# Where a feed-forward pass adds its residual: sixteen half tiles moved from the end of the fourth block to the up projections of the second

## The chip, the cores and the metric

The kernel runs on one core of a Trainium2 chip. The metric is device time in microseconds of one execution; the time before is the median of three runs, 2182.12 us (2181.38 to 2185.97). Five engines work side by side, each through a queue of its own and in that queue's order: TensorE (PE; its weight loads are listed as PEld), VectorE (DVE), ScalarE (ACT), GpSimd (POOL) and SyncE (SP), which here only issues DMA transfers. ACT and POOL can issue transfers too.

## The reference

One layer of an encoder trunk on a sequence of 2048 tokens with 1024 features, float32:

```python
mix, qx = spatial_gating_mixer(x, a_w_in[j], a_v_ln_g[j], a_v_ln_b[j], a_w_s[j], a_b_s[j])
branch = jnp.concatenate([mix, memory_cross_attention(qx, mem, w_mem_kv[i])], axis=-1)
x = layer_norm(DEEPNORM_ALPHA * x + branch @ w_o[i], ln1_g[i], ln1_b[i])
x = layer_norm(DEEPNORM_ALPHA * x + swiglu_ffn(x, ffn_w_in[i], ffn_w_down[i]), ln2_g[i], ln2_b[i])

def swiglu_ffn(x, w_in, w_down):
    h = x @ w_in
    return (jax.nn.silu(h[..., :D_FF]) * h[..., D_FF:]) @ w_down
```

D_FF is 2816, DEEPNORM_ALPHA is 2 to the power 1/4. The change concerns the term `DEEPNORM_ALPHA * x` of the last line, the residual of the feed-forward part (FFN).

## The kernel before, in words

Features lie on the 128 partitions and tokens along the free axis. The first part (mixer, attention, first norm) runs over four chunks of 512 tokens and leaves its result in a DRAM tile `x1d`. Each float32 operand is split into a high part (an ACT cast, L73) and a low part (a DVE subtraction, L74), and each product is three matmuls: high by high, high by low, low by high.

The FFN runs in three passes over 688, 680 and 680 tokens. The 22 tiles of 128 hidden features are taken in five blocks, in passes 1 and 2 of 4, 4, 4, 4 and 6. A block has two stages:

- The up projections (`Pass.up`, matmuls with output h), one for each hidden tile. Each is a seven-product scheme for two by two blocks: products in the order 1, 6, 2, 5, 7, 3, 4, each of 12 matmuls of 340 tokens, each with its own weight w. Four of the seven weights were kept split in DRAM in pass 0 and are loaded (`k_u`, from SP's queue); the other three are loaded as r_u and split anew. After each product comes a "stage" that reads the PSUM bank: L400 after products 1 (ACT) and 6 (DVE), L401 after 2 (ACT) and 5 (DVE), L402 after 7, L392 and others after 3 and 4. Products 3 and 4 go on accumulating in the banks that L401 and L402 have to read first. After a stage, `then` takes steps of generators handed in as `work`: the norm of the pass before (`norm_work`), and `pair`, which splits the results of two finished hidden tiles (gp).
- The down projection. In passes 1 and 2 the first four blocks go through `down7`, again in seven products, on pairs of hidden tiles (matmuls with output e, six to a product): for each of four pairs j of output tiles, products 6, 1, 5, 7 and then, one pair behind, `second` with products 2, 3, 4. DVE adds each product to the pass's accumulators `fa` or to a common term `fu` (L524); in the first block ACT writes some of them instead (L522). In the fourth block (`last`), `second` also adds `fu` to three quarters of the pair (L531, L532) and then the residual: for each of the two output tiles and each half of its tokens, a tile r of 128x340 is loaded from x1d on SP's queue (L539) into the pool `tmp` (nine buffers, which the up projections use as well), and DVE adds ALPHA times r (L541). The fifth block goes through `down` on split results g; then follow the norm and the store.

One up projection of the next block is made before a block's down stage (`ahead`), so four of them stand between the down stages of two blocks.

The order in each engine's queue is planned by the framework when the program is built: it goes by the order in which the program is written and by when it expects operands and buffers to be ready. An instruction can therefore stand in its queue far ahead of others that are written before it. The order of TensorE alone is fixed by hand.

The pool `ln` has one buffer each under the tags s1 and s2. The norm of the second half of a pass's tokens uses them for its sums: from the last down stage of its pass to the up projections of the next pass's first block. GpSimd makes those sums, and in pass 0 it also issues loads of r_es tiles (L481) and stores of weight sums for `left_sums`, a generator whose DVE operations (L493) run between the up projections of pass 0.

Of the kernel before, what the change touches and what calls it, by code (L numbers as in the profile page):

```python
# [11 lines left out]
F32 = mybir.dt.float32  # L12
F32R = mybir.dt.float32r
AF = mybir.ActivationFunctionType
ALU = mybir.AluOpType
AX = mybir.AxisListType

P = 128
# [8 lines left out]
KD = D // P  # L27
# [7 lines left out]
ALPHA = 2.0 ** 0.25  # L35
# [4 lines left out]
def trunk_kernel(ctx, tc, xT, memT, wv, wuq, ws, bs, vg, vb, wmk, wmv, wo,  # L40
                 ln1g, ln1b, w1, w2, ln2g, ln2b, outT):
    nc = tc.nc
# [16 lines left out]
    def matmul(*args, **kw):  # L59
        in_order(nc.tensor.matmul(*args, **kw))  # L60
# [4 lines left out]
    def bank(name):  # L65
        return psum.tile([P, 512], F32, tag="bank", name=name)
# [117 lines left out]
    x1d = dram.tile([D, SEQ], F32, tag="x1d", name="x1d")  # L184
# [108 lines left out]
    def norm_steps(norms, stores, wait, pad):  # L293

        for _ in range(wait):
            yield

        def pairs(call):
            for m in range(0, KD, 2):
                call(m, m + 2)  # L300
                yield

        for x in norms:
            yield from pairs(x.centre)
        for _ in range(pad):
            yield
        for x in norms:
            x.var()
            for _ in range(4):
                yield  # L310
        for _ in range(4):
            yield
        for x, store in zip(norms, stores):
            yield from pairs(lambda a, b: x.finish(store, a, b))
# [12 lines left out]
    open_pools = {}  # L327
# [17 lines left out]
    class Pass:  # L345
# [156 lines left out]
        def down7(self, blk, q, f0, last, w):  # L502

            h, n, gp = self.h, self.n, self.gp
            if blk == 0:
                self.u = [open_pools["sums"].tile([P, 4, P], F32, tag="sums", name=f"fu{self.no}_{m}")
                          .rearrange("p a b -> p (a b)")[:, 0:h] for m in range(0, KD, 2)]
            banks = []

            def product(j, p):  # L510
                y, u = self.out[j], self.u[j]
                c11, c12, c21, c22 = (y[:, a, b * h:(b + 1) * h] for a in range(2) for b in range(2))
                n, start, stop = {1: (0, True, False), 6: (1, True, True), 2: (0, False, True), 5: (2, True, False),
                                  7: (3, True, False), 3: (2, False, True), 4: (3, False, True)}[p]
                bk = banks[j][n]
                for i in range(q):
                    for x, (a, b) in enumerate(PASSES):
                        matmul(bk, w[j][p][:, a, i, :], gp[p][:, i, b], start=start and i == 0 and x == 0,
                               stop=stop and i == q - 1 and x == 2, skip_group_check=True)
                to = {1: u, 6: u, 2: c11, 5: c22, 7: c22, 3: c12, 4: c21}[p]  # L520
                if blk == 0 and p not in (1, 7):
                    nc.scalar.copy(to, bk)  # L522
                else:
                    nc.vector.tensor_add(to, to, bk)  # L524

            def second(j):
                for p in (2, 3, 4):
                    product(j, p)
                if last:
                    y, u = self.out[j], self.u[j]  # L530
                    nc.vector.tensor_add(y[:, 0, h:n], y[:, 0, h:n], u)  # L531
                    nc.vector.tensor_tensor(out=y[:, 1].rearrange("p (b t) -> p b t", b=2),  # L532
                                            in0=y[:, 1].rearrange("p (b t) -> p b t", b=2),
                                            in1=u.unsqueeze(1).broadcast_to([P, 2, h]), op=ALU.add)
                    for m in range(2):
                        m0 = (2 * j + m) * P
                        for x in range(2):
                            r, t0 = self.tmp(f"r{m}{x}_{j}"), self.t0 + x * h
                            nc.sync.dma_start(out=r, in_=x1d[m0:m0 + P, t0:t0 + h])  # L539
                            to = y[:, m, x * h:(x + 1) * h]  # L540
                            nc.vector.scalar_tensor_tensor(out=to, in0=r, scalar=ALPHA, in1=to,  # L541
                                                           op0=ALU.mult, op1=ALU.add)

            for j in range(KD // 2):
                if j < KD // 2 - 1:
                    w.append(self.left(blk, 2 * j + 2, f0, q))
                banks.append([bank(f"e{i}_{self.no}_{blk}_{j}")[:, 0:h] for i in range(4)])
                for p in (6, 1, 5, 7):
                    product(j, p)
                if j:  # L550
                    second(j - 1)
            second(KD // 2 - 1)

        def sums(self):

# [413 lines left out]
    late = chunks[-1]  # L969
# [8 lines left out]
    late.norm.squares = open_pools["sq"]  # L978
    ffn.rest()
    norm_work = norm_steps([late.norm], [late.store], 5, 5)  # L980
    sums_to_make = [(blk, m) for blk in range(4) for m in range(0, KD, 2)]
    for no in range(len(FPASSES)):
        pa, h, n = ffn, FPASSES[no] // 2, FPASSES[no]
        whole = (((h, n), (0, h)),)
        f0 = 0
        blocks = FBLOCKS[no]
        ahead = []

        side = []

        def up(f):
            work = [(norm_work, 1), *side]
            if no == 0 and f > 4 and sums_to_make:
                blk, m = sums_to_make.pop(0)
                work.append((pa.left_sums(blk, m, 4 * blk, 2), 1))
            ys = f, pa.up(f, work)
            for gen, _ in work[1:]:
                for _ in gen:
                    pass
            side.clear()  # L1000
            return ys

        for blk, nb in enumerate(blocks):
            end = blk == len(blocks) - 1
            fs = range(f0 + len(ahead), f0 + nb)
            if no and not end:
                ys = list(ahead)
                for f in fs:
                    ys.append(up(f))
                    if len(ys) % 2 == 0:  # L1010
                        side.append((pa.pair(len(ys) // 2 - 1, blk, ys[-2][1], ys[-1][1]), 2))
                ahead = [up(f0 + nb)]
            else:
                gs = [pa.whole(*y) for y in ahead] + [pa.whole(*up(f)) for f in fs]
                ahead = []
            seven = no and not end
            if seven:
                first = [pa.left(blk, 0, f0, nb // 2)]
            if blk == 0:
                for _ in norm_work:  # L1020
                    pass
                pa.sums()
            if seven:
                pa.down7(blk, nb // 2, f0, blk == len(blocks) - 2, first)
            elif not end:
                pa.down(blk, gs, f0, whole, lambda ci, m: None)
            elif no < len(FPASSES) - 1:
                ffn = Pass(no + 1)
                norms = [pa.norm(0, h), pa.norm(h, n)]

                def done(ci, m):
                    for i in range(2):
                        norms[i].add(pa.ya[m][:, i * h:(i + 1) * h])
                    if m % 2:
                        ffn.load(m // 2)

                pa.down(blk, gs, f0, whole, done)
                norm_work = norm_steps(norms, [pa.store(0, h), pa.store(h, n)], 6, 0)
            else:
                last = (((0, n - 256),), ((n - 256, n),))  # L1040
                norms = [pa.norm(0, n - 256), None]

                def done(ci, m):
                    if ci == 0:
                        norms[0].add(pa.ya[m][:, 0:n - 256])
                    elif m == 0:
                        norms[1] = pa.norm(n - 256, n, True)
                        norms[0].centre(0, 4)
                    else:
                        norms[1].add(pa.ya[m - 1][:, n - 256:n])  # L1050
                        if m == 1:
                            norms[0].centre(4, 8)
                        if m == 5:
                            norms[0].var()
                        if m == 7:
                            norms[0].spread()

                pa.down(blk, gs, f0, last, done)
                norms[1].add(pa.ya[KD - 1][:, n - 256:n])
                norms[1].centre_pairs()  # L1060
                norms[1].var()
                norms[1].spread()
                norms[0].finish(pa.store(0, n - 256))
                norms[1].finish(pa.store(n - 256, n))
            f0 += nb
# [54 lines left out]
```

## Time and profile before

| what | value |
|---|---|
| median of three runs | 2182.12 us |
| lowest and highest | 2181.38, 2185.97 us |
| profiled execution, its own time | 2188.79 us |
| its span | 2186.7 us |
| mean granted TensorE clock | 0.988 |
| busy share of PE, DVE, ACT, POOL | 96%, 73%, 42%, 17% |
| pass 1, first down stage to last up projection | 1320.9 to 1656.4 us |
| pass 2, the same | 1777.9 to 2113.2 us |

Times inside the profile count from the start of the span. A row of the timeline is start, length, engine, line, operation, output and inputs; in brackets stands how long the engine was idle before it, and what ended that. A row of a tile or line gives the number of instructions and their shortest, median and longest duration in ns. "To landing" is the time from the issue of a transfer until its data is there. The granted clock is TensorE's, as a share of full speed.

### The profile page before, as it was taken

How to read it: one execution, taken by the hardware profiler on the slowest of the kernel's cores; microseconds unless marked ns; L12 is line 12 of the kernel's file. 1: busy time of each engine (PE TensorE's matmuls, PEld its weight loads, DVE VectorE, ACT ScalarE, POOL GpSimd, SP SyncE). 2: the span in 40 equal slices, each digit the busy share in tenths (PEclk: the TensorE clock that was granted, in tenths of full speed). 3: DMA queues.
4: the chain of work that ended last, by engine and by line, in shares of the span. 5: the costliest groups of instructions: out<-in, count | busy, mean ns of one | idle time of the engine just before them, and what ended most of it. 6: DMA issues, size and time to landing. Idle time of an engine off the chain costs nothing.

```text
span 2186.7 us, 35143 instructions
## 1 busy us (share of the span) xinstructions
PE 2094.2 (96%) x12938; PEld 1982.2 (91%) x12938; DVE 1606.3 (73%) x3030; ACT 920.8 (42%) x1846; POOL 365.2 (17%) x318
## 2 busy tenths in 40 slices
PE   9899999999999989999999999999999999999896
PEld 7888798788888789999999999999999999999896
DVE  7986796797789796878778885656747755666656
ACT  5553653564474453434434354232224353223234
POOL 0412321331322450001000320000002300000002
PEclk9999999999999999999999999999999999999998
DMA  6233314234333556767668467666754576666652
GB/s 212 78 109 124 115 64 158 97 107 141 129 97 108 171 193 236 251 225 279 231 240 290 163 214 256 218 235 226 269 204 140 200 257 237 232 226 233 241 167 92
DMA packets 158604, 408.13 MB, mean 187 GB/s; under 512 B 15584, under 2 KB 46304, under 8 KB 158432
## 3 DMA queue, kind: packets, MB, share of 16 engines
q1 hardware_dynamic: 138112, 333.50, 45.4%
q10 hardware_dynamic: 12672, 46.14, 5.6%
q0 software_dynamic: 7648, 26.24, 3.4%
q8 instruction: 102, 1.67, 0.3%
q14 instruction: 70, 0.57, 0.1%
HBM read 326.13 MB, written 79.69 MB: 186 GB/s over the span
## 4 chain that ended last, share of the span: by engine, by line
PE 58%; DVE 19%; DMA 10%; ACT 5%; issue 5%; POOL 2%; SPq 0%; ACTq 0%; DVEq 0%; POOLq 0%
PE h L60 31%; PE e L60 9%; PE d L60 8%; PE v L60 5%; PE u L60 3%; DMA r_x<-in_xT 3%; DMA r_f<-x1d 2%; DMA r_es<-in_w 2%; DVE w L74 2%; DVE w_o L74 2%; DVE x L74 1%; DVE w_u L74 1%; POOL s_a L233 1%; ACT p L745 1%; DVE z L702 1%
## 5 line engine op out<-in xcount | busy, mean ns | idle before, releaser
L60 PE MATMUL h<-x,w 128*128 128x340 f32 (+1 forms) x5544 | 888.2, 321 | 37.3 <-DVE w L74 13.9
L60 PEld LDWEIGHTS h<-x,w 128*128 128x128 f32 x5544 | 874.6, 189 | 46.5 <-DVE w L74 15.8
L60 PE MATMUL d<-g,w_d 128*128 128x344 f32 (+3 forms) x1632 | 263.7, 322 | 6.0 <-DVE w_d L74 2.8
L60 PEld LDWEIGHTS d<-g,w_d 128*128 128x128 f32 x1632 | 257.8, 189 | 10.0 <-DVE w_d L74 3.7
L60 PE MATMUL y<-br,w_o 128*128 128x512 f32 x960 | 224.4, 395 | 0.0
L60 PEld LDWEIGHTS y<-br,w_o 128*128 128x128 f32 x960 | 180.4, 188 | 42.1
L60 PE MATMUL e<-gp,w_e 128*128 128x340 f32 x1344 | 211.4, 318 | 0.4 <-DMA w_e<-k_e 0.4
L60 PEld LDWEIGHTS e<-gp,w_e 128*128 128x128 f32 x1344 | 209.9, 188 | 0.8 <-DMA w_e<-k_e 0.7
L60 PE MATMUL v<-w_v,x 128*128 128x512 f32 x768 | 188.2, 401 | 6.6 <-ACT w_v L73 4.8
L73 ACT CAST w<-r_u 128x512 fp32r<-128x512 f32 x198 | 121.8, 618 | 168.2 <-PE h L60 125.0
L74 DVE TENSOR_TENSOR w<-r_u,w 128x512 fp32r<-128x512 f32 x198 | 143.4, 726 | 53.9 <-ACT w L73 46.7
L60 PEld LDWEIGHTS v<-w_v,x 128*128 128x128 f32 x768 | 143.8, 190 | 42.3 <-ACT w_v L73 4.8
L60 PE MATMUL u<-xt,w_u 128*128 128x256 f32 x768 | 97.1, 282 | 0.0
L60 PEld LDWEIGHTS u<-xt,w_u 128*128 128x128 f32 x768 | 94.3, 191 | 0.0
L60 PE MATMUL u<-x,w_u 128*128 128x256 f32 x576 | 79.4, 290 | 12.1 <-DVE u L711 6.2
L369 POOL TENSOR_TENSOR t<-r_f,r_f 128x340 f32<-128x340 f32 (+1 forms) x12 | 14.7, 1227 | 436.7 <-DMA r_f<-x1d 419.9
L60 PEld LDWEIGHTS u<-x,w_u 128*128 128x128 f32 x576 | 72.9, 193 | 14.7 <-issue 6.0
L400 DVE TENSOR_TENSOR u<-h,m 128x340 f32<-128x340 f32 (+1 forms) x66 | 33.7, 511 | 70.7 <-PE h L60 70.3
L73 ACT CAST gp<-c 128x340 fp32r<-128x340 f32 x112 | 51.7, 476 | 74.4 <-DVE c L398 42.0
L74 DVE TENSOR_TENSOR w_o<-r_o,w_o 128x512 fp32r<-128x512 f32 (+1 forms) x96 | 67.3, 712 | 21.0 <-ACT w_o L73 21.0
L73 ACT CAST w_d<-r_d 128x384 fp32r<-128x384 f32 (+2 forms) x104 | 53.2, 519 | 68.9 <-PE d L60 43.7
L74 DVE TENSOR_TENSOR w_d<-r_d,w_d 128x384 fp32r<-128x384 f32 (+2 forms) x104 | 61.9, 599 | 24.5 <-ACT w_d L73 24.3
(212 smaller groups left out, 2873.9 us busy)
## 6 DMA issues: line engine op xcount, KB each, us to landing
w<-k_u SPq DMA_DIRECT2D x176, 512.0 KB, 4.3
r_u<-in_w SPq DMA_DIRECT2D x88, 512.0 KB, 3.5
k_u<-w ACTq DMA_DIRECT2D x88, 512.0 KB, 3.9
r_u<-in_wuq SPq DMA_DIRECT2D x32, 512.0 KB, 3.3
r_o<-in_wo SPq DMA_DIRECT2D x32, 512.0 KB, 3.5
r_e<-in_w SPq DMA_DIRECT2D x64, 256.0 KB, 3.0
w_e<-k_e SPq DMA_DIRECT2D x64, 256.0 KB, 3.7
w_e<-k_e SPq DMA_DIRECT2D x32, 512.0 KB, 4.5
```

What stands on the lines that cost most here:

```text
L60: in_order(nc.tensor.matmul(*args, **kw))
L73: nc.scalar.copy(hi, src)
L74: engine.tensor_sub(lo, src, hi.bitcast(F32))
L233: nc.gpsimd.tensor_add(self.s2, self.s2, sq)
L369: nc.gpsimd.tensor_sub(t3, b22, b12)
L400: stages = {1: lambda: nc.scalar.copy(m1, q0), 6: lambda: nc.vector.tensor_add(u2, q1, m1), 2: lambda: nc.scalar.activation(m1, q0, AF.Sil ...
L702: nc.vector.tensor_scalar(z[h][:, b], z[h][:, b], mv[:, b, 0:1], rs[:, b:b + 1], ALU.subtract, ALU.mult)
L745: nc.scalar.activation(pr[:, h, :], svs[h // 2][:, h % 2, :], AF.Exp, scale=HD ** -0.5, bias=mxv[:, h:h + 1], accum_out=sm[:, h:h + 1])
```

## The change

The residual leaves `second` of the fourth block. A new generator `residual` loads each half tile from x1d on GpSimd's queue into the buffers s1 and s2 of the pool `ln` in turn, and adds ALPHA times it to the accumulator two loads later. It is created after the down stage of the first block, and one step of it is taken after each stage of the up projections that follow, behind the step of `norm_work`. Sixteen loads and two closing steps fit into the 28 stages of four up projections; what is left would be done ahead of the down stage of the third block. It holds for passes 1 and 2; pass 0 adds its residual with the first down products, as before.

```diff
@@ down7, second @@
-                    for m in range(2):
-                        m0 = (2 * j + m) * P
-                        for x in range(2):
-                            r, t0 = self.tmp(f"r{m}{x}_{j}"), self.t0 + x * h
-                            nc.sync.dma_start(out=r, in_=x1d[m0:m0 + P, t0:t0 + h])
-                            to = y[:, m, x * h:(x + 1) * h]
-                            nc.vector.scalar_tensor_tensor(out=to, in0=r, scalar=ALPHA, in1=to,
-                                                           op0=ALU.mult, op1=ALU.add)
@@ Pass @@
+        def residual(self):
+            h, late = self.h, []
+
+            def add():
+                to, r = late.pop(0)
+                nc.vector.scalar_tensor_tensor(out=to, in0=r, scalar=ALPHA, in1=to, op0=ALU.mult, op1=ALU.add)
+
+            for m in range(KD):
+                for x in range(2):
+                    if len(late) == 2:
+                        add()
+                    r = open_pools["ln"].tile([P, 432], F32, tag=f"s{1 + x}", name=f"res{self.no}_{m}_{x}")[:, 0:h]
+                    t0 = self.t0 + x * h
+                    nc.gpsimd.dma_start(out=r, in_=x1d[m * P:(m + 1) * P, t0:t0 + h])
+                    late.append((self.ya[m][:, x * h:(x + 1) * h], r))
+                    yield
+            while late:
+                add()
+                yield
@@ the loop over passes and blocks @@
+    residual = iter(())
...
-            work = [(norm_work, 1), *side]
+            work = [(norm_work, 1), (residual, 1), *side]
...
-            for gen, _ in work[1:]:
+            for gen, _ in work[2:]:
...
+            if blk == 2:
+                for _ in residual:
+                    pass
...
                 pa.down7(blk, nb // 2, f0, blk == len(blocks) - 2, first)
+                if blk == 0:
+                    residual = pa.residual()
```

## The prediction

> **What bounds the kernel now.** I read the page first, for the engine that sets the time.
>
> ```profile
> span 2186.7 us, 35143 instructions
> PE 2094.2 (96%) x12938; PEld 1982.2 (91%) x12938; DVE 1606.3 (73%) x3030; ACT 920.8 (42%) x1846; POOL 365.2 (17%) x318
> ```
>
> TensorE (PE) is busy 96% of the span, so a change pays only where PE stands still or runs slowly. The moved work sits in passes 1 and 2, at the end of their fourth block. There I read the chain of waits in order of time (start, length, what), from block 2 on.
>
> ```profile
> 1478.12 26.19 PE e L60 x168
> 1504.31 52.39 PE h L60 x336
> ...
> 1586.13 1.77 DVE fa L541 x4
> 1587.90 0.85 DVE g L74 x2
> 1588.75 0.61 DVE w L74
> 1589.41 61.62 PE h L60 x382
> ```
>
> Block 2 runs without a gap: 168 down products (e) in 26.19, then four up projections (h, 336 matmuls) in 52.39, so 0.1559 us a matmul. Block 3 does not: between e and h stand four residual adds (L541), two splits of g, and the split of the next weight w, which PE needs. The timeline of PE gives the sizes, pass 1 first, then pass 2 (start, length, what, and in brackets the idle time before it).
>
> ```profile
> 1556.54 10.46 PE L60 MATMUL e<-gp,w_e 128*128 128x340 f32 x66
> 1567.38 16.18 PE L60 MATMUL e<-gp,w_e 128*128 128x340 f32 x102 [0.38 <-DMA w_e<-k_e]
> 1583.39 0.47 PE L60 MATMUL h<-x,w 128*128 128x340 f32 x2
> 1589.41 67.21 PE L60 MATMUL h<-x,w 128*128 128x340 f32 x418 [5.55 <-DVE w L74]
> ...
> 2013.59 26.38 PE L60 MATMUL e<-gp,w_e 128*128 128x340 f32 x168
> 2039.81 0.47 PE L60 MATMUL h<-x,w 128*128 128x340 f32 x2
> 2045.82 67.57 PE L60 MATMUL h<-x,w 128*128 128x340 f32 x418 [5.54 <-DVE w L74]
> ```
>
> Each pass idles 5.5 us for that split. The stretches in time show a second loss (columns: length, then busy time of PE, PEld, DVE, ACT and POOL, granted clock, DMA share, GB/s).
>
> ```profile
> 1320.92:1347.14 26.22, 26.22 (x170) 26.22 (x170) 10.40 (x23) 13.09 (x31) 0.00 (x0) 1.00 0.70 235
> 1347.14:1399.52 52.38, 52.38 (x338) 52.38 (x338) 30.07 (x59) 18.28 (x39) 0.00 (x0) 1.00 0.67 232
> 1478.12:1504.31 26.19, 26.19 (x171) 26.19 (x170) 19.42 (x42) 5.08 (x12) 0.00 (x0) 1.00 0.66 219
> 1556.70:1583.60 26.90, 26.52 (x170) 26.22 (x169) 24.17 (x54) 5.37 (x13) 0.00 (x0) 1.00 0.92 297
> 1583.60:1589.40 5.80, 0.26 (x2) 0.00 (x0) 5.80 (x14) 0.00 (x0) 0.00 (x0) 0.75 0.65 254
> 1589.40:1593.40 4.00, 3.99 (x14) 3.99 (x15) 0.56 (x1) 0.44 (x1) 0.00 (x0) 0.51 0.36 131
> 2045.82:2049.82 4.00, 4.00 (x14) 4.00 (x15) 0.54 (x1) 0.44 (x1) 0.00 (x0) 0.50 0.36 131
> ```
>
> VectorE (DVE) is busy 24.17 of 26.90 in block 3's down stage and all of the 5.80 behind it: a backlog. For 4 us after the idle time the granted clock is half. DMA share is 0.92 there against 0.66 in block 2.
>
> **The cost of the stall as it stands.** Pass 1: idle 5.55; the 418 matmuls should take 418 x 0.1559 = 65.2 and took 67.2, so 2.0; the e stage from 1556.54 to 1583.39 is 26.85 against 26.19, so 0.7. Pass 2: 5.54, and 67.57 - 65.2 = 2.4; its e stage lost nothing. Together 8.2 + 7.9 = 16.1 us. This is the most that this part can return, 0.74%.
>
> [...]
>
> **Removed from block 3.** These rows are the residual tiles' own (durations in ns: least, median, most).
>
> ```profile
> L539 SPq DMA_DIRECT2D r<-x1d x32: 319/402/1167, 1557.3 to 2037.2; - x32
> L541 DVE SCALAR_TENSOR_TENSOR fa<-r,fa x32: 502/504/511, 1565.9 to 2043.8; 128x340 f32<-128x340 f32 x32
> DMA to landing us min/median/max: 3.1/4.8/6.1
> ```
>
> L539 is the load, L541 the add. Per pass, 16 loads leave SP's queue (16 x 0.40 = 6.4 us of issuing), 2.8 MB leave a stretch whose DMA share was 0.92, and 16 adds leave DVE. Overlapped, four adds take 1.77 us, so 0.44 each and 7.1 us in all. DVE's work from 1556.70 to the last split was 24.17 + 5.80 = 30.0 us; without the adds 22.9, against 26.2 us of PE. The backlog of 5.5 us is smaller than the 7.1 taken out. The 0.38 us wait for w_e, behind the r loads on SP's queue, goes too.
>
> What is late next: after the last product an add, the two u sums (L531 and L532), g and w still follow in before's order. The first row is L532's group within the backlog (count, busy time, mean ns); the second is a w split of block 2 on DVE's timeline.
>
> ```profile
> L532 DVE TENSOR_TENSOR fa<-fa,fu 128x680 f32<-128x680 f32 x1 | 0.9, 859 | 0.0
> ```
>
> ```profile
> 1497.70 0.69 DVE L74 TENSOR_TENSOR w<-r_u,w 128x512 fp32r<-128x512 f32 x1
> ```
>
> If w stays last, PE waits for 0.50 + 0.43 + 0.78 + 0.85 + 0.61 = 3.2 us less the 0.3 us of its two free matmuls, 2.9. If w is queued as in block 2, where it ran at 1497.70, 6.6 us ahead of the stage's end, PE waits for nothing. The queues aren't in program order (w is written after those products), and w goes into a gap of DVE. With 22.9 of 26.2 us used, block 3 has gaps as block 2 has (19.42). I take 0.9 a pass, one L532 ahead of w; bounds 0 and 2.9.
>
> **Added to the up projections of block 1.** POOL issues 16 loads a pass, where it has nothing else to do (0.00 busy in the stretch 1347.14:1399.52). At 546 ns, by the r_es row below, that is 8.7 us, and nothing is queued behind them: after the norm's last sums in block 0, POOL's next work is at the end of the pass.
>
> ```profile
> 1655.51 1.15 POOL L369 TENSOR_TENSOR t<-r_f,r_f 128x340 f32<-128x340 f32 x1 [376.61 <-DMA r_f<-x1d]
> ```
>
>  The buffers s1 and s2 are free by then: the norm that uses them ends in block 0. DVE gets 7.1 us, 30.1 + 7.1 = 37 of 52.4. DMA gets 2.8 MB on 12.2 MB (52.4 us at 232 GB/s), so the share goes from 0.67 to about 0.82; PE's weight loads bore 0.92 in block 3 with 0.38 us lost, so I take zero, bounds 0 and 0.4 a pass.
>
> The price is a wait on DVE. Two buffers serve 16 loads, so each buffer makes 8 rounds: add, load, landing, add. In program order an add stands two steps of 12 matmuls after its load, 2 x 1.87 = 3.74 us. If the load comes later, DVE, which runs in order, stands still, and PE's stages behind it too. Before has one like case: in pass 0, r_es tiles are loaded from GpSimd's queue and used by DVE between up projections.
>
> ```profile
> L481 POOL DMA_DIRECT2D r_es<-in_w x32: 543/546/576, 823.4 to 1176.5; - x32
>   DVE s_es L493: 9.0, 5
> DMA to landing us min/median/max: 3.8/6.7/8.9
> ```
>
> ```profile
> PE h L60 <- DVE c L401: 4.5, 4, 1.8
> ```
>
> There DVE waited 5 times in 16, 9.0 us in all, and PE lost 4.5 us, behind L401; 0.28 us a round. What DVE can wait without harm is seen in block 1's rows.
>
> ```profile
> 1354.65 0.51 DVE L401 TENSOR_TENSOR c<-h,u 128x340 f32<-128x340 f32 x1 [0.18 <-PE h L60]
> 1356.52 0.51 DVE L402 TENSOR_TENSOR c<-h,c 128x340 f32<-128x340 f32 x1 [1.35 <-PE h L60]
> ```
>
> Each must end before the product after next, 1.87 us after its start is possible: 1.87 - 0.51, less 0.2 for handing over (an estimate, from the 0.18 in the row), leaves 1.1 us. With landing at 4.8 (the r row) a round is 4.8 + 0.5 for the add + 0.1 = 5.4, 1.7 over the two steps and 0.6 over the slack. With 6.7 (the r_es row) it is 7.3, 2.4 over. With 3.1 nothing is lost. 8 rounds a pass lie between 0 and 8 x 2.4 = 19 us. I take r_es's 0.28 a round, since there DVE and PE stand in the same pattern and the queue is the same: 16 x 0.28 = 4.5 for two passes. Half of that falls away, as the first two loads have their buffers long before and the adds of early tiles can go into block 0's down stage, where DVE idles 26.22 - 10.40 = 15.8 us: 2.3.
>
> [...]
>
> **Sum.** 16.1 returned, less 2 x 0.9 at the tail, less 2.3 in the up projections: 12.0 us. The profiled execution took 2188.8 (2186.7 span), 0.3% above the median 2182.1 of the three runs; the difference carries over. 2182.1 - 12.0 = 2170.
>
> **The rivals.** (a) All of it comes back: w is early, and the loads are hidden in block 0 and the norm's free buffers. 2182.1 - 16.1 = 2166. For it: DVE's free 15.8 us; against: adds cannot precede their tiles, which end through the whole of block 0's down stage.
>
> (b) The change moves the backlog but w stays last in its queue. Then PE still waits 2.9 us a pass; 5.8 lost of 16.1, and 2.3 in the ups; if the clock also drops, 2.0 more a pass. 2174 to 2178. For it: the planned order of before put w behind all of DVE's late work. Against: three blocks of before put w ahead.
>
> (c) Slower: GpSimd's loads land late in every round, with all 16 in the up projections. One mechanism, DVE standing at the add with L401 or L402 behind it. At 7.3 us a round it costs 38 us and the kernel takes 2182.1 - 16.1 + 1.8 + 38 = 2206; if half the rounds go into block 0's stage, 2187. It decides at (16.1 - 1.8)/16 = 0.9 us lost a round, a landing of 0.9 + 1.1 + 3.74 - 0.6 = 5.1 us. For it: the r_es median lies above, and its rounds here come back to back. Against: r_es loads were queued behind 512 KB stores and each other, these are one at a time.
>
> (d) No change: the same mechanism with landings near 5.1 in all rounds, or near 6.0 in half of them: 2178 to 2186.
>
> **How the numbers follow.** Forecast 0.50; (a) 0.15; (b) 0.12; (d) 0.11; (c) 0.12. 0.2% of this kernel, 4.4 us, is about what a measurement can tell from no change. Forecast, (a) and (b) are faster, 0.77, of which I give 0.02 to the same: 0.75, 0.13, 0.12. The range goes from the full return, 2165, to 2183, leaving out (c) and the upper half of (d). The forecast's own range is 2167 to 2175.
>
> **What would show it.** Right: no gap over 1 us on PE between the fourth block's e stage and the next h in passes 1 and 2, the granted clock at 1.00 there, DVE's w split ahead of the last adds, and the up projections of block 1 at 52 to 55 us. Wrong: DVE idle with the residual load as its releaser before the new add, over 1 us each and many of them, with PE waiting on L401, L402 or w within 1347 to 1399 of pass 1 and the like stretch of pass 2; or the 5.5 us gap still there.

## The result: slower by 1%, and the profile after

The changed kernel takes 2203.45 us (median of four runs, 2202.19 to 2206.85) against 2183.97 us before; the ratio is 1.0097, 95% interval 1.0083 to 1.0111. In a later comparison it was 1.0085 (1.0070 to 1.0100). The forecast was 2170.

The profiled execution took 2202.19 us, its span is 2200.4. Work per engine is what it was: the page has PE at 2097.0 us busy (2094.2 before), DVE at 1607.9 (1606.3). What changed is where PE stands still. First the place that the residual left: the timeline of PE around the fourth block of pass 1 (start, length, what; idle time before it in brackets).

```profile
1569.23 26.38 PE L60 MATMUL e<-gp,w_e 128*128 128x340 f32 x168
1595.45 65.65 PE L60 MATMUL h<-x,w 128*128 128x340 f32 x420
1660.94 2.67 PE L60 MATMUL d<-g,w_d 128*128 128x340 f32 x16
```

No gap is left: 26.2 and 65.5 us where before had 26.9 and 73.1, and 26.2 and 65.4 in pass 2 (26.2 and 73.4 before). The two passes together got 16.3 us back. DVE's timeline shows why PE did not wait.

```profile
1589.93 0.69 DVE L74 TENSOR_TENSOR w<-r_u,w 128x512 fp32r<-128x512 f32 x1
...
1595.51 0.52 DVE L531 TENSOR_TENSOR fa<-fa,fu 128x340 f32<-128x340 f32 x1
1595.94 0.50 DVE L524 TENSOR_TENSOR fa<-fa,e 128x340 f32<-128x340 f32 x1
1596.47 0.87 DVE L532 TENSOR_TENSOR fa<-fa,fu 128x680 f32<-128x680 f32 x1
```

The split of w stands 5.5 us ahead of the stage's end, with the last adds and sums behind it. Now the place that the residual came to: the timeline of PE in block 1 of pass 1, then in pass 2.

```profile
1318.98 17.01 PE L60 MATMUL e<-gp,w_e 128*128 128x340 f32 x108
1336.33 6.78 PE L60 MATMUL e<-gp,w_e 128*128 128x340 f32 x42 [0.34 <-DMA w_e<-k_e]
1345.00 3.07 PE L60 MATMUL e<-gp,w_e 128*128 128x340 f32 x18 [1.89 <-DVE fu L524]
1347.91 7.65 PE L60 MATMUL h<-x,w 128*128 128x340 f32 x48
1357.33 3.67 PE L60 MATMUL h<-x,w 128*128 128x340 f32 x12 [1.77 <-DMA w<-k_u]
1367.12 45.10 PE L60 MATMUL h<-x,w 128*128 128x340 f32 x276 [6.12 <-DVE c L401]
...
1807.97 4.61 PE L60 MATMUL e<-gp,w_e 128*128 128x340 f32 x18 [2.14 <-DVE fu L524]
1812.41 7.62 PE L60 MATMUL h<-x,w 128*128 128x340 f32 x48
1820.26 2.13 PE L60 MATMUL h<-x,w 128*128 128x340 f32 x12 [0.23 <-DMA w<-k_u]
1831.05 45.16 PE L60 MATMUL h<-x,w 128*128 128x340 f32 x276 [8.66 <-DVE c L401]
```

PE waits for L401, the read that a product needs to go on, 6.1 and 8.7 us (the number in brackets). The four up projections last 64.1 and 63.6 us instead of 52.4 and 52.3, and the down stage ahead of them 28.9 and 30.6 instead of 26.2 and 26.3. Lost: 11.7 + 11.3 + 2.7 + 4.3 = 30.0 us. Against the 16.3 that is 13.7, the difference of the two spans (2200.4 - 2186.7). The medians differ by 19.5; the rest is that before's profiled execution lay 4.8 us above the median and this one 1.3 below.

What held L401 is seen on DVE in the same 12 us.

```profile
1355.27 0.51 DVE L553 SCALAR_TENSOR_TENSOR fa<-res,fa 128x340 f32<-128x340 f32 x1 [5.08 <-DMA res<-x1d]
1357.03 0.51 DVE L553 SCALAR_TENSOR_TENSOR fa<-res,fa 128x340 f32<-128x340 f32 x1 [1.25 <-DMA res<-x1d]
1360.37 0.51 DVE L553 SCALAR_TENSOR_TENSOR fa<-res,fa 128x340 f32<-128x340 f32 x1 [2.82 <-DMA res<-x1d]
1361.03 0.51 DVE L553 SCALAR_TENSOR_TENSOR fa<-res,fa 128x340 f32<-128x340 f32 x1
1361.46 0.50 DVE L400 TENSOR_TENSOR u<-h,m 128x340 f32<-128x340 f32 x1
1361.88 0.68 DVE L74 TENSOR_TENSOR w<-r_u,w 128x512 fp32r<-128x512 f32 x1
1364.10 0.51 DVE L553 SCALAR_TENSOR_TENSOR fa<-res,fa 128x340 f32<-128x340 f32 x1 [1.53 <-DMA res<-x1d]
1365.54 0.51 DVE L553 SCALAR_TENSOR_TENSOR fa<-res,fa 128x340 f32<-128x340 f32 x1 [0.92 <-DMA res<-x1d]
1365.97 0.68 DVE L74 TENSOR_TENSOR w<-r_u,w 128x512 fp32r<-128x512 f32 x1
1366.57 0.50 DVE L401 TENSOR_TENSOR c<-h,u 128x340 f32<-128x340 f32 x1
```

The adds stand ahead of L400 and L401 in DVE's queue, and DVE stands at each add until its load lands. L400's input had been there since 1351.7, two products after 1347.91. The tile's own view sums this up (issues; then what ended idle time before an add, total and times; then from issue to landing; rows between are left out).

```profile
L561 POOL DMA_DIRECT2D res<-x1d x32: 536/538/583, 1266.2 to 1825.2; - x32
...
  DMA res<-x1d: 53.4, 24
DMA to landing us min/median/max: 2.5/3.7/6.5
```

DVE waited 53.4 us in 24 of the 32 adds. The landings themselves are quick, a median of 3.7 us, less than the 4.8 of before's r tiles. This is the sign of being wrong that the prediction had named: DVE idle with the residual load as its releaser, 2.2 us on the mean, and PE behind L401.

### The profile page after: what moved, and what is told of

Its sections match the earlier page's. It is cut to its first block, busy times and chain, and to the rows that moved or that the text cites. A ratio compares the mean times of both kernels' runs of the same rounds, so it can differ in the third digit from the quotient of the medians.

```text
span 2200.4 us, 35159 instructions
## 1 busy us (share of the span) xinstructions
PE 2097.0 (95%) x12938; PEld 1984.1 (90%) x12938; DVE 1607.9 (73%) x3030; ACT 920.4 (42%) x1846; POOL 382.2 (17%) x350
## 4 chain that ended last, share of the span: by engine, by line
PE 58%; DVE 18%; DMA 10%; issue 7%; ACT 4%; POOL 3%; ACTq 0%; DVEq 0%; SPq 0%; POOLq 0%
PE h L60 29%; PE d L60 9%; PE e L60 8%; PE v L60 5%; PE u L60 3%; DMA res<-x1d 2%; DMA r_es<-in_w 2%; DMA r_x<-in_xT 2%; PE y L60 2%; DVE w L74 2%; DVE w_o L74 1%; DVE w_u L74 1%; DMA r_f<-x1d 1%; DVE x L74 1%; POOL s_a L233 1%
## 5 line engine op out<-in xcount | busy, mean ns | idle before, releaser
L74 DVE TENSOR_TENSOR w<-r_u,w 128x512 fp32r<-128x512 f32 x198 | 143.4, 725 | 52.4 <-ACT w L73 45.6
L524 DVE TENSOR_TENSOR fa<-fa,e 128x340 f32<-128x340 f32 x128 | 64.5, 506 | 23.3 <-PE e L60 21.1
L74 DVE TENSOR_TENSOR w_d<-r_d,w_d 128x384 fp32r<-128x384 f32 (+2 forms) x104 | 61.8, 598 | 26.6 <-ACT w_d L73 26.4
L73 ACT CAST w_e<-r_e 128x256 fp32r<-128x256 f32 x96 | 35.8, 405 | 102.4 <-PE e L60 77.3
```

Of the source, the lines that this page charges most:

```text
L73: nc.scalar.copy(hi, src)
L74: engine.tensor_sub(lo, src, hi.bitcast(F32))
```

## The experiments

Theory R: an add waits for a load that could only be issued when the add before it, in the same buffer, was done; with two buffers such rounds (add, issue, landing, next add in the same buffer) are too long for the pace that the program sets, two steps of 12 matmuls or 3.74 us a round. Rivals: D, the adds' own time on DVE; C, the loads' traffic; Q, loads from GpSimd's queue are slow. Later P: the place of the adds in DVE's queue decides, and the choice of the queue acts through that place.

The table has block 1 of passes 1 and 2 from each profile's PE timeline: the down stage ahead of the up projections, then the four up projections, in us. Ratios are against before, beside it on the same chip.

| kernel | down stages | up projections | ratio, 95% interval |
|---|---|---|---|
| before | 26.2, 26.3 | 52.4, 52.3 | |
| changed | 28.9, 30.6 | 64.1, 63.6 | 1.0097 (1.0083 to 1.0111) |
| no residual | 26.2, 26.2 | 52.4, 52.3 | 0.9936 (0.9916 to 0.9957) |
| two loads | 26.2, 26.2 | 52.4, 52.3 | 0.9936 (0.9919 to 0.9954) |
| four buffers | 27.2, 26.3 | 54.0, 54.4 | 0.9957 (0.9942 to 0.9971) |
| SyncE's queue | 26.4, 26.2 | 55.9, 56.9 | 0.9963 (0.9946 to 0.9980) |
| pinned adds | 26.2, 26.2 | 63.0, 62.8 | 1.0021 (1.0008 to 1.0034) |
| SyncE's queue, early adds | 26.2, 26.2 | 64.7, 66.7 | 1.0040 (1.0026 to 1.0054) |
| four buffers, pinned | 26.2, 26.2 | 54.6, 54.2 | 0.9948 (0.9927 to 0.9968) |
| preloaded accumulators | 31.7, 33.3 | 52.4, 52.3 | 0.9979 (0.9968 to 0.9989) |
| half pace, pinned | 26.2, 26.2 | 52.4, 52.3 | 0.9939 (0.9918 to 0.9959) |
| four buffers, SyncE's queue | 26.2, 26.2 | 54.2, 53.9 | 0.9950 (0.9935 to 0.9965) |
| changed, again | 30.2, 28.9 | 63.3, 65.3 | 1.0085 (1.0070 to 1.0100) |

The diffs below are against the changed kernel and shortened; `...` stands for what is left out.

**No residual.** What leaves block 3, the fourth, is priced alone.

```diff
-                    residual = pa.residual()
+                    residual = iter(())
```

> Leaves out the residual of passes 1 and 2 altogether (no loads, no adds). It prices what left block 3. All theories: the 16.1 us read off the trace of before come back, 2184 - 16 = 2168 us (2166 to 2170). If the block's stall had another cause than the residual, it stays near 2184.

2172.07 us against 2186.53, ratio 0.9936: 14 us. The 16 that were expected (0.9926) lie within the interval; the time itself is above the expected 2170 because before took 2186.5 beside it and not 2184. The stall of block 3 was the residual's.

**Two loads.** All adds, nearly no loads: 14 of a pass's 16 adds take rows that were loaded for the first two.

```diff
-                    r = open_pools["ln"].tile(...)
...
-                    nc.gpsimd.dma_start(out=r, in_=x1d[...])
+                    if m == 0:
+                        r = open_pools["ln"].tile(...)
...
+                        nc.gpsimd.dma_start(out=r, in_=x1d[...])
+                        held.append(r)
+                    r = held[x]
```

> The changed kernel, but only the first two half tiles are loaded in each pass; the other 14 adds read these again (so they add the wrong rows). 16 adds, 2 loads. Theory R (VectorE stands at the add for a load that could be issued only after the add before it): the loss goes, 2167 to 2171 us. Rival D (the adds' own VectorE time ahead of the up projections' stages): stays at 2200 to 2204. Rival C (the loads' traffic delays weight loads): 2167 to 2171 as well.

The same 2172.07 us (1 us above R's range) and 0.9936, and no time lost in block 1. Sixteen adds a pass cost nothing there, though the plan put all of them ahead of the first L400; D is out. R and C are left.

**Four buffers.**

```diff
-                    if len(late) == 2:
+                    if len(late) == 4:
...
-                    r = open_pools["ln"].tile([P, 432], F32, tag=f"s{1 + x}", ...)
+                    r = (open_pools["ln"].tile([P, 432], F32, tag=f"s{1 + x}", ...) if m % 2 else
+                         open_pools["sq"].tile([P, 512], F32, tag="squares", ...))
```

> The changed kernel with four buffers instead of two (two more from the norm's squares) and the add four loads behind. Same loads, same adds, half as many rounds. R: the changed kernel lost 19.5 + 16 = 35 us in 16 rounds, 2.2 us each; 8 rounds cost 18 us, so 2168 + 18 = 2186 us (2175 to 2190). C: the same traffic, closer together, 2200 us or more. D: 2200 to 2204.

0.9957, faster than before and better than R's size: about 5 us lost in block 1 instead of 30, with the same traffic. C is out as the main cause; a little of it may be left, for all of PE's waits there are for weight loads (1.6 us in pass 1, 1.4 in pass 2). The tile's view:

```profile
  DMA res<-x1d: 27.2, 17
DMA to landing us min/median/max: 2.6/5.6/7.2
```

DVE still waits 27.2 us and the landings are slower (a median of 5.6 us against 3.7), but the adds, all 16 ahead of the first L400, are over before PE needs L401.

**SyncE's queue.**

```diff
-                    nc.gpsimd.dma_start(out=r, in_=x1d[m * P:(m + 1) * P, t0:t0 + h])
+                    nc.sync.dma_start(out=r, in_=x1d[m * P:(m + 1) * P, t0:t0 + h])
```

> The changed kernel with the 16 loads issued from SyncE's queue. R: the round is the same length, so 2195 to 2215 us, the upper end because weight loads now stand behind loads that wait for a buffer. Rival Q (loads from GpSimd's queue are what is slow): most of the loss goes, 2170 to 2180 us.

0.9963: R's expectation failed, Q's was met. But the landings don't bear Q out.

```profile
L561 SPq DMA_DIRECT2D res<-x1d x32: 319/326/782, 1264.8 to 1816.2; - x32
  DMA res<-x1d: 21.6, 18
DMA to landing us min/median/max: 2.8/3.8/7.3
```

3.8 us against 3.7. What differs is DVE's queue. With GpSimd's loads the plan put 14 of a pass's 16 adds ahead of the first L400 of block 1; with SyncE's, 8, and the others one by one between the stages of the first two up projections. So P, and two runs that part queue and place.

**Pinned adds.** GpSimd's queue, but each add has an ordering edge behind the last of DVE's PSUM reads so far. (`marks` is the list of those reads, `behind` makes the edge; both are added elsewhere in the edit.)

```diff
-                nc.vector.scalar_tensor_tensor(out=to, in0=r, scalar=ALPHA, ...)
+                behind(nc.vector.scalar_tensor_tensor(out=to, in0=r, scalar=ALPHA, ...), marks[-1])
```

> GpSimd's queue and two buffers as in the changed kernel, but each add is held in VectorE's queue behind the PSUM read of the stage at which the program asks for it, so that none stands ahead of its place. Theory P (what costs is where the plan put the adds: 14 of 16 ahead of the first up projection's read L400, at rounds shorter than the real ones of 4.5 to 7 us; the queue only decides the plan): ratio 0.994 to 0.998, 2171 to 2180 us against 2184, since a round of 4.5 us is 0.8 over the two steps and the slack is 1.1. Rival Q (loads from GpSimd's queue are slow in themselves): 1.005 or more, 2195 us.

1.0021, between P's range and Q's. The down stage is whole again, but the up projections lose 10.6 and 10.5 us. The PE timeline of pass 1:

```profile
1359.91 5.86 PE L60 MATMUL h<-x,w 128*128 128x340 f32 x36 [0.64 <-ACT m L408]
1369.69 14.91 PE L60 MATMUL h<-x,w 128*128 128x340 f32 x84 [3.92 <-DVE c L409]
1386.79 15.38 PE L60 MATMUL h<-x,w 128*128 128x340 f32 x87 [2.19 <-DVE c L409]
```

(L408 and L409 are L400 and L401 here.) P's estimate, like the prediction, had let the slack of 1.1 us cover each round anew. But a late add makes the next load late, and what is over adds up.

**SyncE's queue, early adds.** The plan's place under GpSimd's queue, forced on SyncE's; `first_up` has the next L400 held behind the add made last, the fourteenth.

```diff
                     residual = pa.residual()
+                    for _ in range(16):
+                        next(residual)
+                    first_up.append(True)
...
```

> SyncE's queue as in the run before it, but 14 of the 16 adds are written ahead of the first up projection and its read L400 is held behind the fourteenth: the changed kernel's order with the other queue. P: the loss comes back, ratio 1.005 to 1.012, 2195 to 2210 us, with PE idle 5 us or more for L401 in each pass. Q: it stays where SyncE's queue was, 0.995 to 0.998.

1.0040, just under P's lower end, and the up projections are as bad as the changed kernel's. Same queue, same loads and landings as in the run "SyncE's queue"; only the place of the adds is another. PE in pass 1 (L414 is L401 here), and the loads:

```profile
1366.96 44.99 PE L60 MATMUL h<-x,w 128*128 128x340 f32 x276 [10.42 <-DVE c L414]
```

```profile
DMA to landing us min/median/max: 2.3/3.7/6.3
```

Q is out. An early place alone costs nothing or little, as the kernels with two loads and with four buffers show, where all 16 adds stand ahead of L400; it costs where a round is long against the pace. In the changed kernel the down stage lost 7.0 us besides; here it lost nothing.

**How long a round is.** The adds of one buffer, first and last of pass 1, in the changed kernel, in the pinned one and in this last:

```profile
1328.07 0.51 DVE L553 SCALAR_TENSOR_TENSOR fa<-res,fa 128x340 f32<-128x340 f32 x1 [0.17 <-ACT fa L522]
1364.10 0.51 DVE L553 SCALAR_TENSOR_TENSOR fa<-res,fa 128x340 f32<-128x340 f32 x1 [1.53 <-DMA res<-x1d]
```

```profile
1346.71 0.50 DVE L561 SCALAR_TENSOR_TENSOR fa<-res,fa 128x340 f32<-128x340 f32 x1
1384.60 0.51 DVE L561 SCALAR_TENSOR_TENSOR fa<-res,fa 128x340 f32<-128x340 f32 x1 [0.34 <-DMA res<-x1d]
```

```profile
1329.91 0.51 DVE L566 SCALAR_TENSOR_TENSOR fa<-res,fa 128x340 f32<-128x340 f32 x1 [0.17 <-ACT fa L535]
1364.34 0.51 DVE L566 SCALAR_TENSOR_TENSOR fa<-res,fa 128x340 f32<-128x340 f32 x1 [1.29 <-DMA res<-x1d]
```

Seven rounds each: 36.0, 37.9 and 34.4 us, so 5.1, 5.4 and 4.9 a round, with either queue and in either place. With pinned adds two steps allow 3.74: 37.9 - 7 x 3.74 = 11.7, less the slack of 1.1 once, is 10.6, and 10.6 were lost in this pass. That the two agree so closely is luck. In pass 2 the seven rounds take 36.5 us and the same sum gives 9.2, where 10.5 were lost; only 18 of the 32 pinned adds waited for a load, the others for their stage; and by PE's rows the 10.6 are 6.75 us of idle time and, behind the two longer gaps, some 1.7 us each of slow clock (granted 0.57 in the 4 us behind either).

**Four buffers, pinned.** The edits of "Four buffers" and "Pinned adds" together; a round may last 4 steps.

> GpSimd's queue, four buffers, adds held behind their stages: each add 4 steps (7.5 us) behind its load. P and R: no wait is left, as with two loads only: ratio 0.993 to 0.9945, 2168 to 2172 us. Q with slow loads of over 7.5 us: 1.000.

0.9948, just above the expected range, which lies inside its interval. 2.2 and 1.9 us are still lost in the up projections, and all of PE's waits there are for weight loads (w, 1.3 and 1.1 us), which fits a small part of C.

**Preloaded accumulators.** No separate add: block 0's first write to each quarter is ALPHA times the preloaded accumulator plus the product.

```diff
-                if self.no == 0:
-                    nc.sync.dma_start(out=y, in_=two_tiles(x1d, m, self.t0, self.n))
+                queue = nc.gpsimd if self.no else nc.sync
+                queue.dma_start(out=y, in_=two_tiles(x1d, m, self.t0, self.n))
...
-                if blk == 0 and p not in (1, 7):
+                if blk == 0 and p == 6:
                     nc.scalar.copy(to, bk)
+                elif blk == 0 and p not in (1, 7):
+                    nc.vector.scalar_tensor_tensor(out=to, in0=to, scalar=ALPHA, in1=bk, ...)
...
-                    residual = pa.residual()
+                    residual = iter(())
```

> Another way to the same result without separate adds: in passes 1 and 2 the accumulators are loaded with the residual rows before block 0's down stage (four loads a pass, GpSimd's queue), and block 0's first write to each quarter is a VectorE operation ALPHA times accumulator plus PSUM instead of ScalarE's copy. 16 adds fewer on VectorE, 16 copies fewer on ScalarE. If the loads are there in time: ratio 0.993, 2168 us. They can only be issued when the last norm's stores have read the buffers, some 10 us ahead of their use: if they are late, PE stands in block 0's down stage, 3 to 8 us a pass, 0.996 to 1.000.

0.9979. The up projections are whole, but block 0's down stage loses 5.5 and 7.0 us. The late loads that were feared are in the trace: DVE stands 3.6 and 3.0 us for an accumulator's load (`fa<-x1d`). PE itself waits for weights w_e, 4.7 and 4.1 us in all; one of their loads is issued only after DVE's add behind that wait.

**Half pace.** The pinned kernel with two buffers, one load in every second stage, over blocks 1 and 2 (the edit of "Pinned adds" is in it).

```diff
                     late.append((self.ya[m][:, x * h:(x + 1) * h], r))
                     yield
+                    yield
...
-            if blk == 2:
+            if blk == 3:
                 for _ in residual:
```

> GpSimd's queue, two buffers, adds held behind their stages as in the run with the pinned order, but one load in every second stage, so the 16 are spread over the up projections of blocks 1 and 2. Same loads, same buffers, same adds; only the pace differs: a buffer's round has four steps, 7.5 us, instead of 3.74. Theory R with numbers (a round of add, load, landing takes 5.1 us in the changed kernel and 5.4 with pinned adds, whatever the queue; what is over the allowed time adds up round by round): no loss, ratio 0.993 to 0.995, 2168 to 2173 us, and up projections of block 1 within 1 us of 52.4. If a load from GpSimd's queue disturbed the up projections in another way, the loss stays, spread over two blocks: 1.000 to 1.002.

2170.59 us against 2184.79, ratio 0.9939, as R expected and as fast as without any residual. Block 2, which takes the rest of the loads, loses 0.5 us in one pass and nothing in the other.

```profile
1340.97 52.55 PE L60 MATMUL h<-x,w 128*128 128x340 f32 x336
```

```profile
  DMA res<-x1d: 3.3, 2
DMA to landing us min/median/max: 2.5/4.2/5.7
```

Same queue, buffers, loads and adds, landings no shorter (a median of 4.2 us against 3.6), and DVE's wait falls from 28.5 us in the pinned kernel to 3.3. The pace was the cause. Of the versions that keep the whole residual it has the lowest ratio, clear of before and of the changed kernel; the intervals of the versions with four buffers overlap with its own.

**Four buffers on SyncE's queue.** The edits of "Four buffers" and "SyncE's queue" together.

> Four buffers, SyncE's queue, adds where the plan puts them. R: four loads in flight and a plan that allows more for each: ratio 0.993 to 0.995, the loss against no residual under 3 us. If SyncE's queue holds weight loads back behind loads that wait for a buffer: 0.996 to 0.999.

2174.42 us, 0.9950 (0.9935 to 0.9965), the upper end of R's range: no better than four buffers pinned on GpSimd's. PE waits here for L402, 1.55 and 1.30 us.

**The changed kernel again.** No edit.

> The changed kernel once more, beside these two: 1.008 to 1.011, with the up projections of block 1 near 64 us in both passes.

2203.14 us, 1.0085 (1.0070 to 1.0100), with PE idle 7.69 us for L401 in pass 1.

## Why the prediction was wrong

- **The return from block 3** (16.1 us): right, 16.3 by the stages and 14 by the run without a residual. The bound on the tail (0 to 2.9 a pass, 0.9 taken) holds at its lower end: w went ahead of the last adds, as in block 2, so rival (b) did not happen.
- **The adds' DVE time and the traffic** (zero): right for the adds, as the two-loads kernel shows. For the traffic nearly: weight loads held PE 1.77 and 0.23 us in the up projections and 0.34 and 0.16 in the down stages, where 0 to 0.4 a pass was the bound.
- **The length of a round** (5.4 us from the r row): right in sum, 5.1, with luck in the parts: a landing of 4.8 and 0.6 beside it were taken. The loads of the changed kernel that follow an add landed in 4.3 on the mean, and some 0.9 lies beside them.
- **The failed step** is the price of those rounds: "I take r_es's 0.28 a round", and then half of it, 2.3 us for both passes, where 30.0 were lost. Three things in it were wrong. First, the r_es loads are used one up projection after another; 13 us or more lie between the issues of one pair and the next, and behind the uses that waited longest (1.7 to 2.9 us) the next did not wait. Here each load starts from the add before it, so what is over the pace adds up; the working beside it that counted 0.6 us a round "over the slack" spent the same 1.1 us in every round. Second, I read the plan's freedom to move adds into block 0's down stage as cover ("Half of that falls away"). It moved 14 of 16 ahead of the first L400, and with rounds of 5.1 us that is where DVE then stood, L400 some 10 us behind its input; early adds against spaced ones on the same queue are 64.7 and 66.7 us against 55.9 and 56.9. Third, the slow clock after such gaps was not in the sum (2.0 us behind the gap of 6.12, by the first row in the last section).
- **Rival (c)** named the place, DVE standing at the add with L401 behind it, and its 2206 us lies near 2203. Its price was right in size by luck: it took landings of 6.7 us, and their median was 3.7. Its point of decision, a landing of 5.1 us, is refuted: landings were below it and the kernel was slower. What decides is a round over the pace.
- **The down stage of block 0** was to give cover; it lost 7.0 us in the changed kernel and none with SyncE's queue and early adds. The planned orders differ in a few places: in the changed kernel three residual adds in a row stand ahead of a sum that PE needs (L524), with SyncE's queue two. DVE in pass 1:

```profile
1344.01 0.51 DVE L553 SCALAR_TENSOR_TENSOR fa<-res,fa 128x340 f32<-128x340 f32 x1 [4.01 <-DMA res<-x1d]
1344.44 0.50 DVE L524 TENSOR_TENSOR fu<-fu,e 128x340 f32<-128x340 f32 x1
```

The third add waits 4.0 us for its load with that L524 behind it, and PE's row at 1345.00 has waited 1.89 for L524 (2.14 in pass 2, with slow clock behind it). Why the plans differ there is not known.

## What to carry to other kernels

A ring of n buffers that is refilled only after its consumer has run sets a pace of one round through n; take the round from two uses of one buffer in the trace, compare it with the step that the consumer should keep, and count what is over once for every round, the slack once in all (here 10.6 and 9.2 us, where 10.6 and 10.5 were lost). Where the order of an in-order queue is planned, an instruction that may move early can also stand early: ask who is behind it. Here doubling the steps between loads was as good as having no loads at all (0.9939 against 0.9936), and cost no buffer.

## What the runs showed of the hardware

**The granted clock fell behind gaps of 2.14 and 2.19 us, as it had behind those of 5.5 in before (0.50 and 0.51), and the length of the gap alone did not tell where.** These stretches of 4 us follow a gap on PE; the columns are those of the prediction's stretches, the granted clock third from the end. The first two are of the changed kernel, after gaps of 6.12 and 2.14 us.

```profile
1367.12:1371.12 4.00, 4.00 (x14) 4.00 (x15) 1.30 (x3) 0.00 (x0) 0.00 (x0) 0.50 0.35 131
```

```profile
1807.97:1811.97 4.00, 4.00 (x16) 4.00 (x17) 3.25 (x7) 0.73 (x2) 1.35 (x3) 0.57 0.32 89
```

In the pinned kernel, after 2.19 us:

```profile
1386.79:1390.79 4.00, 4.00 (x16) 4.00 (x17) 1.81 (x4) 0.00 (x0) 0.00 (x0) 0.57 0.74 242
```

With SyncE's queue, after 2.06 us (idle for L400 on ACT):

```profile
1363.79:1367.79 4.00, 4.00 (x25) 4.00 (x26) 3.96 (x10) 2.94 (x7) 0.00 (x0) 1.00 0.60 235
```

Gaps of 2.14 and 2.19 us had 4 us at little over half speed behind them (0.57), 1.7 us lost each time (0.43 of 4 us); 2.06 had none (1.00). But 2 us is no limit. With SyncE's queue the 48 matmuls behind a gap of 1.78 us in pass 2 (from 1807.82) took 9.27 us, where the 48 from 1347.91 of the changed kernel took 7.65; in the changed kernel the 4 us behind a gap of 2.50 us, which ends at 1314.00, were at 1.00. What tells such gaps apart was not shown.

**A load from GpSimd's queue landed as soon as one from SyncE's:** 3.7 us against 3.7 and 3.8 (medians, 174 KB). The issue itself took longer on GpSimd's, 0.54 us against 0.32 and 0.33. And a landing is not a round: 4.3 for the landing on the mean of those that follow an add (2.5 to 6.5), 0.5 for the add, 0.3 until the next issue begins (add ends 1348.52, load issued 1348.82) and 0.1 from landing to add make the 5.1 to 5.2.
